# A hybrid encoder layer: value tiles in the pool of the FFN's activations, two gates as a pair at the joint, attention outputs on the other side of memory

## The chip, the core and the metric

The kernel runs on one core of a Trainium2 chip. The core has a matrix engine (PE, its weight loads PEld), a vector engine (DVE), an activation engine (ACT), a general engine (POOL) and a queue engine (SP). Each takes its instructions in the order in which they were written; they wait for each other by semaphores. SP and POOL issue the transfers (DMA) between the device's memory and the 128 partitions of the core's own memory, and a waiting transfer holds back all that stands behind it on its engine. The metric is the device time of one execution in microseconds. Of the kernel before, three runs took 1272.62, 1275.5 and 1276.87 us, so the median is 1275.5 us.

## The reference

One encoder layer over 512 tokens of 1024 features, in float32:

```python
x = x + 0.5 * swiglu(rmsnorm(x, ffn1_norm), w1, w3, w2)     # FFN a, 2816 hidden
h = rmsnorm(x, mix_norm)
proj = h @ w_in                 # q, k, v of attention A | q, k, v of attention B | gates
o_a = dilated attention, 24 heads of 64 in 3 groups (dilation 1, 4, 16), relative bias,
      the groups combined by their softmax denominators
o_b = attention with 8 query heads of 128 and 2 key heads, normalised q and k, rotary
merged = sigmoid(g_A) * (o_a @ w_branch_a) + sigmoid(g_B) * (o_b @ w_branch_b)
x = x + merged @ w_out
x = x + 0.5 * swiglu(rmsnorm(x, ffn2_norm), ...)            # FFN b
return rmsnorm(x, final_norm)
```

## The kernel before

The 512 tokens stand as columns, the features in eight tiles of 128 partitions (x0 to x7). Every product keeps float32 precision: an operand is split into a rounded part H and a remainder L, and `mm3` (L254) makes three matmuls of them, H·H, H·L and L·H. A weight tile of 512 KB is loaded raw (wr; wt, wa and ws for the Strassen products), ACT rounds it (wh<-..., L241), and DVE takes the remainder (wl<-..., L242). A product of one weight tile with all tokens ("feature piece", `feat`, L266) takes 24 matmuls of 512 columns. A part of the FFNs and of the projection uses Strassen's scheme (`strassen`, L308): a group of four blocks becomes seven products (A11, S1, S2, A12, S3, S4, A22) of 24 matmuls of 256 columns each. For S1 and S3 the raw weight wt is the sum of two blocks, and the second is added by a transfer that accumulates, issued on POOL (L223); for S2 and S4 DVE adds two tiles (ws<-..., L240).

PE's instructions stand in the order of the program. Other engines' instructions are placed by a scheduler, within the dependences. Tiles live in pools that are opened and closed like brackets; a pool opened where another lay waits, tile by tile, for the last reader of what lay there.

The stages in order: FFN a; the projection for attention A ("sw", ten tiles of q and k as five groups f = 0, 2, ..., 8 and the values as three groups f = 10, 12, 14) with a gate piece ahead of it; attention A with the remaining projection pieces woven in as filler (`stream`, L642; `weave`, L390); attention B with more filler; the branch products and the output projection (wo); FFN b.

**Joint 1**, FFN a to the projection. FFN a's last product, over the tiles d in the order ROWS = (0, 4, 1, 5, 2, 6, 3, 7), adds to x[d]; then ACT makes hH[d] (L398) and DVE hL[d] (L399), the normalised operand without the factor 1/rms, and the squares are summed in acc. `then(gp)` runs the projection (`project_qk`, L722) while the FFN's pools are still open. It starts with the first gate through `feat`, k = 0 to 7, whose result stays in its bank. Then follow the product A11, `stat_r` (L418, the sum of acc over the partitions, and the power -0.5 on POOL, L416), the next product, and `stat_R` (L427), which spreads the factors to R; then the gate is scaled and stored to `gate_d`.

**Joint 2**, the projection to attention A. The evictions write q and k to the device's memory `qk_d` (L746) and the values to `v_d` (L762), through two staging tiles qo. The groups of values come last (f = 10, 12, 14). `mixer` then opens a pool V (two value tiles, on the right), the pool oA of attention A's outputs, and the pool A, with the third value tile, the q and k tiles of a head pair (qk) and the probabilities. `fetch(0)` (L685) loads q and k of the first head pair, and `fetch_v` (L687 to L690) the three value tiles of 1 MB, all on POOL's queue. SP loads the bias tables W (L823, L824). Head pair by head pair, `scores_a` makes S on PE (L850) and P = S + W with its row maximum MX on DVE (L855); `values_a` follows a pair later.

**FFN b's opening.** The output projection's operands mH and mL lie in the pool M. FFN b's pools open behind it. Before, its raw weights wt and wa lay where attention A's and B's tiles had lain, apart from mH and mL.

Of the kernel before, what the change touches and what calls it, by code (L numbers as in the profile page):

```python
# [24 lines left out]
NSQ = 10  # L25
NSW = NSQ + 6
# [12 lines left out]
T = 512  # L39
# [34 lines left out]
class Layer:  # L74
    def __init__(self, ctx, tc, a):
# [34 lines left out]
        for kind, n in self.items:  # L110
            if kind == "sw":
                self.order += [("swq", at) for at in self.slots(range(0, NSW, 2), True)]
# [65 lines left out]
    def offset(self, n):  # L178
        name, key = self.order[n][:2]
        if name[:2] == "sw":  # L180
            return 160 - 128 * (n % 2)
        if name == "w2b" and key >= (NF + GROUPS["b"][2]) // 2:
            return 96
        return 160 if name in ("w2a", "w2b", "wpa", "wpb", "wo") else 224
# [91 lines left out]
    def pair(self, name, done):  # L276
        ws = [self.weights(name, c) for c in range(2)]
        banks = [self.bank() for _ in ws]
        for k in range(NK):
            s = slice(128 * k, 128 * k + 128)  # L280
            for c, (H, L) in enumerate(ws):
                self.mm3(banks[c], H[:, s], L[:, s], self.hH[k], self.hL[k], k == 0, k == NK - 1)
                if k == NK - 1:
                    done[c](banks[c])
                yield
# [153 lines left out]
    def ffn(self, s, gin, gnext, hooks, out=None, side=None, then=None):  # L439
        with ExitStack() as ctx:  # L440
# [201 lines left out]
    def stream(self, items, held=None):  # L642
        nc = self.nc
        later = lambda fn: fn if held is None else lambda ps: held.append((fn, ps))
        for kind, n in items:
# [11 lines left out]
            elif kind == "g":  # L657

                def done(ps, j=n):
                    z = self.tmp.tile([128, T], F32, tag="t", name="z")  # L660
                    nc.vector.tensor_mul(z, ps, self.R)
                    nc.sync.dma_start(self.gate_d[j], z)

                yield from self.feat("wg", n, later(done))
# [21 lines left out]

    def fetch_v(self):  # L687
        for g in range(3):
            rows = self.v_d[g].rearrange("(m r) f -> m r f", r=4) if g else self.v_d[g].rearrange("(i p) f -> p i f", p=128)
            self.nc.gpsimd.dma_start(self.V[g], rows)  # L690
# [31 lines left out]
    def project_qk(self, gp):  # L722
        nc, cp = self.nc, self.cp
        if True:
            held = []
            for _ in self.stream(self.items[:self.head], held):
                pass
            c, turn = {}, itertools.count()
# [19 lines left out]
            def staged():  # L748
                return self.g_tile(gp, next(turn) % 2, "qo", F32)[:, :1024]

            def tokens(o, src, half, neg):
                for j in range(2):
                    i = 2 * half + j
                    out, part, rc = o[:, 256 * i:256 * i + 256], src[:, 256 * j:256 * j + 256], self.r[:, i:i + 1]
# [5 lines left out]
            def store_v(f, at, o):  # L760
                dst = self.v_d[(f - NSQ) // 2].rearrange("(i p) f -> p i f", p=128)
                nc.gpsimd.dma_start(dst[:, :, at:at + 256], o.rearrange("p (i f) -> p i f", i=4))  # L762

            def evict(f, step, ps):
# [15 lines left out]
                elif step == "S4":  # L780
                    nc.vector.tensor_add(hi, ps, hi)
                    o = staged()
                    if f >= NSQ:
                        tokens(o, lo, 0, False)
                        tokens(o, hi, 1, False)
                        store_v(f, 0, o)
                        return
# [3 lines left out]
                elif f >= NSQ:  # L791
                    o = staged()
                    tokens(o, ps, 0, True)
                    tokens(o, c2, 1, True)
                    store_v(f, 256, o)
# [6 lines left out]
            def settle():  # L802
                self.stat_R()
                for fn, ps in held:
                    fn(ps)
# [87 lines left out]
    def values_a(self, hp, P, F):  # L893
# [17 lines left out]
        for stage in range(4):  # L911
# [153 lines left out]
    def mixer(self):  # L1065
        nc, tc = self.nc, self.tc
        vctx = ExitStack()
        vp = vctx.enter_context(tc.tile_pool(name="V", bufs=1, side="right", reuse_waits="tile"))
        self.V = [vp.tile([128, 4, 512], F32, name=f"V{g}") for g in range(2)]
        fill = self.stream(self.items[self.head + 1:])  # L1070
        with tc.tile_pool(name="oA", bufs=1, reuse_waits="tile") as oa:
            self.oH = [oa.tile([128, T], F32R, name=f"oH{h}") for h in range(4)]
            self.oL = [oa.tile([128, T], F32R, name=f"oL{h}") for h in range(4)]
            with tc.tile_pool(name="A", bufs=1, reuse_waits="tile") as ap:
                self.ap = ap
                self.V.append(ap.tile([128, 4, 512], F32, name="V2"))
                self.fetch(0)
                self.fetch_v()
# [16 lines left out]
            vctx.close()  # L1095
# [188 lines left out]
```

## Time and profile before

| | |
|---|---|
| median of three runs | 1275.5 us |
| profiled execution, its own time | 1272.24 us |
| its span | 1270.5 us |
| granted PE clock, mean | 0.992 |
| bytes moved | 192.95 MB, 152 GB/s |
| DVE, ACT, POOL busy | 72%, 48%, 10% |

The span is the time from the first to the last instruction of the profiled execution; 1.7 us lie around it. A row of a timeline gives the start, the duration, the engine, the line of the kernel, the operation, and out<-in by the program's names; in brackets stands the idle time before it and what ended it. A row of windows gives, for each engine, busy time and number of instructions, then PE's granted clock, the busy share of the DMA engines and GB/s.

The chain that ended last belongs to PE nearly throughout:

```profile
PE 91%; DVE 4%; DMA 2%; issue 1%; ACT 1%; SPq 0%; POOL 0%; POOLq 0%; DVEq 0%
```

### The profile page before, as it was taken

What the parts mean: (1) busy time and instruction counts of PE and PEld (TensorE: products, weight loads), DVE (VectorE), ACT (ScalarE), POOL (GpSimd) and SP (SyncE); (2) the same over time, 40 slices, a digit from 0 to 9 for tenths busy, and PEclk for the clock granted to TensorE, in tenths of its full rate; (3) what the DMA queues carried; (4) which work ended last, traced back from release to release, by engine and by line L of the source; (5) the groups of instructions that cost most, each with busy time, mean ns of one, the idle gap of its engine ahead of it and who ended that gap; (6) DMA issues with size and microseconds to landing.
All of it is one profiled execution on the core that took longest, in us unless ns stands there. A gap on an engine that the chain in (4) does not pass through costs nothing.

```text
span 1270.5 us, 20497 instructions
## 1 busy us (share of the span) xinstructions
PE 1242.5 (98%) x8214; PEld 1107.6 (87%) x8214; DVE 917.2 (72%) x1372; ACT 605.3 (48%) x903; POOL 131.2 (10%) x139
## 2 busy tenths in 40 slices
PE   9999999999999999699999999999999999999997
PEld 7897999899889999477788878888889989988996
DVE  7784687569988886366746798856777747874775
ACT  8551354155554445354423446655465415532553
POOL 1111110001212110310000200000301000100001
PEclk9999999999999999899999999999999999999998
DMA  9875766367369873853223220147837636743222
GB/s 299 232 187 177 189 187 181 98 168 198 100 147 258 249 200 113 302 168 102 76 104 108 83 92 26 34 142 215 223 101 199 183 94 176 194 150 106 62 82 67
DMA packets 88271, 192.95 MB, mean 152 GB/s; under 512 B 12768, under 2 KB 19312, under 8 KB 87920
## 3 DMA queue, kind: packets, MB, share of 16 engines
q1 hardware_dynamic: 68336, 142.32, 33.5%
q0 software_dynamic: 19120, 48.78, 18.3%
q8 instruction: 64, 1.05, 0.3%
q10 hardware_dynamic: 720, 0.55, 0.1%
q14 instruction: 31, 0.25, 0.1%
HBM read 176.84 MB, written 18.43 MB: 154 GB/s over the span
## 4 chain that ended last, share of the span: by engine, by line
PE 91%; DVE 4%; DMA 2%; issue 1%; ACT 1%; SPq 0%; POOL 0%; POOLq 0%; DVEq 0%
PE mm L256 23%; PE mm L257 22%; PE mm L258 22%; PE Y L257 4%; PE Y L256 4%; PE Y L258 4%; PE X L256 2%; PE X L257 2%; PE X L258 2%; PE S L850 1%; PE mm L901 1%; DMA qk<-qk_d 1%; PE Tb L1040 1%; PE T L919 1%; DVE wl L242 1%
## 5 line engine op out<-in xcount | busy, mean ns | idle before, releaser
L241 ACT CAST wh<-wr 128x1024 fp32r<-128x1024 f32 x133 | 139.4, 1049 | 178.4 <-PE mm L257 126.5
L256 PE MATMUL mm<-hH,wh 128*128 128x256 f32 (+1 forms) x600 | 201.4, 336 | 2.0 <-ACT hH L398 1.9
L257 PE MATMUL mm<-hL,wh 128*128 128x256 f32 (+1 forms) x600 | 196.6, 328 | 1.1 <-DVE hL L399 1.0
L258 PE MATMUL mm<-hH,wl 128*128 128x256 f32 (+1 forms) x600 | 196.4, 327 | 0.9 <-DVE wl L242 0.9
L242 DVE TENSOR_TENSOR wl<-wr,wh 128x1024 fp32r<-128x1024 f32 x133 | 163.0, 1226 | 29.3 <-ACT wh L241 28.9
L256 PE MATMUL mm<-gg,wh 128*128 128x512 f32 (+1 forms) x376 | 141.5, 376 | 0.0
L257 PE MATMUL mm<-gg,wh 128*128 128x512 f32 (+1 forms) x376 | 141.0, 375 | 0.0
L258 PE MATMUL mm<-gg,wl 128*128 128x512 f32 (+1 forms) x376 | 141.0, 375 | 0.0
L256 PEld LDWEIGHTS mm<-hH,wh 128*128 128x128 f32 x600 | 113.4, 189 | 17.9 <-issue 3.7
L257 PEld LDWEIGHTS mm<-hL,wh 128*128 128x128 f32 x600 | 113.6, 189 | 11.6 <-DVE hL L399 2.6
L258 PEld LDWEIGHTS mm<-hH,wl 128*128 128x128 f32 x600 | 113.2, 189 | 11.9 <-DVE wl L242 1.3
L257 PE MATMUL mm<-TL,wh 128*128 128x256 f32 x384 | 106.0, 276 | 0.0
L258 PE MATMUL mm<-TH,wl 128*128 128x256 f32 x384 | 106.0, 276 | 0.0
L256 PE MATMUL mm<-TH,wh 128*128 128x256 f32 x384 | 106.0, 276 | 0.0
L241 ACT CAST wh<-wa 128x1024 fp32r<-128x1024 f32 x54 | 56.8, 1051 | 96.0 <-PE mm L257 48.3
L241 ACT CAST wh<-ws 128x1024 fp32r<-128x1024 f32 x54 | 56.8, 1052 | 76.6 <-PE mm L257 49.2
L242 DVE TENSOR_TENSOR wl<-wt,wh 128x1024 fp32r<-128x1024 f32 x54 | 66.1, 1224 | 34.5 <-ACT wh L241 33.6
L529 DVE TENSOR_TENSOR u<-mm,R 128x512 f32<-128x512 f32 (+1 forms) x52 | 33.7, 648 | 79.2 <-PE mm L258 79.0
L241 ACT CAST wh<-wt 128x1024 fp32r<-128x1024 f32 x54 | 56.8, 1052 | 67.0 <-PE mm L257 39.8
L242 DVE TENSOR_TENSOR wl<-wa,wh 128x1024 fp32r<-128x1024 f32 x54 | 67.0, 1241 | 27.5 <-ACT wh L241 27.5
L256 PEld LDWEIGHTS mm<-gg,wh 128*128 128x128 f32 x376 | 70.6, 188 | 14.1 <-PE mm L258 0.9
L258 PEld LDWEIGHTS mm<-gg,wl 128*128 128x128 f32 x376 | 70.6, 188 | 12.9
(261 smaller groups left out, 3209.2 us busy)
## 6 DMA issues: line engine op xcount, KB each, us to landing
wr<-in_w2a SPq DMA_DIRECT2D x22, 512.0 KB, 3.7
wr<-in_w2b SPq DMA_DIRECT2D x22, 512.0 KB, 3.5
wt<-in_w13b SPq DMA_DIRECT2D x20, 512.0 KB, 4.1
wa<-in_w13b SPq DMA_DIRECT2D x20, 512.0 KB, 3.4
wt<-in_w13b POOLq DMA_DIRECT2D x20, 512.0 KB, 5.8
wt<-in_w13a SPq DMA_DIRECT2D x18, 512.0 KB, 3.5
wt<-in_w13a POOLq DMA_DIRECT2D x18, 512.0 KB, 6.0
wa<-in_w13a SPq DMA_DIRECT2D x18, 512.0 KB, 3.5
```

The source lines that it names most:

```text
L241: self.nc.scalar.copy(H, raw)
L242: self.nc.vector.tensor_sub(L, raw, f32(H))
L256: mm(out, lH, rH, start=start, stop=False, skip_group_check=more)
L257: mm(out, lH, rL, start=False, stop=False, skip_group_check=more)
L258: mm(out, lL, rH, start=False, stop=stop, skip_group_check=more)
L529: nc.vector.tensor_mul(u, ps, R)
L850: nc.tensor.matmul(*args, start=True, stop=True)
L901: nc.tensor.matmul(oc, v, p, start=st, stop=sp)
L919: nc.tensor.transpose(ps[:, 128 * b:128 * b + 128], P[h][:, c0 + 128 * b:c0 + 128 * b + 128], self.ident)
L1040: nc.tensor.transpose(pt[:, 128 * j:128 * j + 128], P[h, j][:, 128 * k:128 * k + 128], self.ident)
```

## The change

It has three parts, and their tiles move in memory with them.

1. At joint 1 gates 0 and 1 run as a pair (`pair` gets the order of k as an argument, here ROWS), both results stay in their banks, `stat_r` follows directly, and after the first product `settle` makes R and scales both gates. Gate 1 leaves the filler of attention A.
2. The projection takes the values of groups 12 and 14 first, then q and k, then group 10 (`SW_Q`). The pool g, which held FFN a's activations, stays open until attention A ends (`gctx`) and holds the value tiles: V1 and V2, stored to `v_d` and read back as soon as both halves are there, and V0, which the evictions write in place. The two staging tiles become two halves of one tile. The transposed probabilities PT lie in pool g too. `fetch_v` and the pool V are gone.
3. The pool oA goes to the right end of memory; pool g lies below wx and c in both FFNs, and the tiles of the attentions lie elsewhere in consequence. FFN b's wt and wa now lie where mH and mL lie.

```diff
-NSW = NSQ + 6
+SW_Q = (NSQ + 2, NSQ + 4, *range(0, NSQ, 2), NSQ)
...
-        self.v_d = self.dram.tile([3, T, 512], F32, name="v_d")
+        self.v_d = self.dram.tile([2, T, 512], F32, name="v_d")
...
-        self.items = (gates(0, 1) + [("sw", 0)] + gates(1, 5) + [("qk", f) for f in range(NSQ, 12)]
+        self.items = (gates(0, 2) + [("sw", 0)] + gates(2, 5) + [("qk", f) for f in range(NSQ, 12)]
...
-            at[1] = at.pop(6)
+            at[1], at[2], at[3] = at.pop(6), at.pop(7), at.pop(2)
...
-    def pair(self, name, done):
+    def pair(self, name, done, ks=range(NK)):
...
-            self.wx = self.shifted(pool("wx", bufs=1), 128)
-            self.cp = self.shifted(pool("c", bufs=2), 128)
-            gp = pool("g", bufs=1)
+            if then:
+                self.gctx = ExitStack()
+                gp = self.gctx.enter_context(self.tc.tile_pool(name="g", bufs=1, reuse_waits="tile"))
+            else:
+                gp = pool("g", bufs=1)
+            self.wx = self.shifted(pool("wx", bufs=1), 64)
+            self.cp = pool("c", bufs=2)
...
-            for _ in self.stream(self.items[:self.head], held):
+            hold = lambda j: lambda ps: held.append((j, ps))
+            for _ in self.pair("wg", [hold(j) for j in range(self.head)], ROWS):
                 pass
+            self.stat_r()
+            self.V = {g: self.g_tile(gp, g, f"V{g}", F32).rearrange("p (i f) -> p i f", i=4) for g in (1, 2)}
+            both = self.g_tile(gp, 0, "qo", F32)
...
+            def values(f, at, a, b, neg):
+                g = (f - NSQ) // 2
+                if g == 0 and at == 0:
+                    self.V[0] = self.g_tile(gp, 0, "V0", F32).rearrange("p (i f) -> p i f", i=4)
+                o = staged().rearrange("p (i f) -> p i f", i=4) if g else self.V[0][:, :, at:at + 256]
+                tokens(o, a, 0, neg)
+                tokens(o, b, 1, neg)
+                if g:
+                    d = self.v_d[g - 1]
+                    nc.gpsimd.dma_start(d.rearrange("(i p) f -> p i f", p=128)[:, :, at:at + 256], o)
+                    if at:
+                        nc.gpsimd.dma_start(self.V[g], d.rearrange("(m r) f -> m r f", r=4))
...
-            hooks = {0: self.stat_r, 1: settle, 3: self.stat_p}
-            for n, _ in enumerate(self.strassen("q", range(0, NSW, 2), evict)):
+            hooks = {0: settle, 2: self.stat_p}
+            for n, _ in enumerate(self.strassen("q", SW_Q, evict)):
                 if n in hooks:
                     hooks[n]()
             self.TQ = None
+            self.PT = self.g_tile(gp, 3, "PT", F32)
...
-                pt = ap.tile([128, T], F32, tag="PT", name="PT", bufs=4)
+                at = T * (2 * (stage % 2) + h)
+                pt = self.PT[:, at:at + T]
...
-        vp = vctx.enter_context(tc.tile_pool(name="V", bufs=1, side="right", reuse_waits="tile"))
-        self.V = [vp.tile([128, 4, 512], F32, name=f"V{g}") for g in range(2)]
...
-        with tc.tile_pool(name="oA", bufs=1, reuse_waits="tile") as oa:
+        with tc.tile_pool(name="oA", bufs=1, side="right", reuse_waits="tile") as oa:
...
-                self.V.append(ap.tile([128, 4, 512], F32, name="V2"))
                 self.fetch(0)
-                self.fetch_v()
...
-            vctx.close()
+            self.gctx.close()
```

What this moves on the engines, at three places. The first is PE at joint 1, at the first gate's first matmuls; hH and hL are the eight operand tiles, mm the banks. Before:

```order
L256 MATMUL mm_3497<-hH0_97,wh_3356 128x512
L257 MATMUL mm_3497<-hL0_105,wh_3356 128x512
L258 MATMUL mm_3497<-hH0_97,wl_3357 128x512
L256 MATMUL mm_3497<-hH1_98,wh_3356 128x512
L257 MATMUL mm_3497<-hL1_106,wh_3356 128x512
L258 MATMUL mm_3497<-hH1_98,wl_3357 128x512
L256 MATMUL mm_3497<-hH2_99,wh_3356 128x512
```

Of the change:

```order
L256 MATMUL mm_3506<-hH0_97,wh_3357 128x512
L257 MATMUL mm_3506<-hL0_105,wh_3357 128x512
L258 MATMUL mm_3506<-hH0_97,wl_3358 128x512
L256 MATMUL mm_3507<-hH0_97,wh_3394 128x512
L257 MATMUL mm_3507<-hL0_105,wh_3394 128x512
L258 MATMUL mm_3507<-hH0_97,wl_3395 128x512
L256 MATMUL mm_3506<-hH4_101,wh_3357 128x512
```

Each operand tile now serves two banks, mm_3506 and mm_3507, before the next one is touched, and tile 4 comes where tile 1 came.

The second place is POOL's queue from the last groups of the projection to the first fetches of attention A (qk_d and v_d are in the device's memory, in_wav are weights). Before:

```order
L746 DMA qk_d<-qo 128x2x512 x2
L223 DMA wt<-in_wav 128x1024
L762 DMA v_d<-qo 128x4x256 x5
L690 DMA V_5404<-v_d 128x4x512
L762 DMA v_d<-qo 128x4x256
L690 DMA V_5405<-v_d 128x2048
L685 DMA qk<-qk_d 128x512 x6
L690 DMA V_5420<-v_d 128x2048
```

Of the change, the same engine from the first group of q and k on:

```order
L771 DMA v_d<-qo 128x4x256 x2
L223 DMA wt<-in_waq 128x2x512
L773 DMA V_3564<-v_d 128x2048
L223 DMA wt<-in_waq 128x2x512
L771 DMA v_d<-qo 128x4x256 x2
L223 DMA wt<-in_waq 128x2x512
L773 DMA V_3565<-v_d 128x2048
...
L747 DMA qk_d<-qo 128x2x512 x2
L223 DMA wt<-in_wav 128x1024
L747 DMA qk_d<-qo 128x2x512 x4
L687 DMA qk<-qk_d 128x512 x20
```

The loads of V now stand among the projection's accumulating weight transfers, there are two instead of three, and the fetches of qk follow the stores of qk directly.

The third place is DVE at FFN b's opening, from the last tile of the sum of squares on; ms<-stat takes the statistics, T, TH and TL are Strassen's sums of the operand. Before:

```order
L409 TENSOR_TENSOR acc<-acc,sq 128x512
L366 TENSOR_TENSOR T_9263<-T_9263 128x1024
L415 TENSOR_SCALAR ms<-stat 128x4
L242 TENSOR_TENSOR wl<-wr,wh 128x1024
L366 TENSOR_TENSOR T_9263<-T_9264,T_9263 128x1024
L359 TENSOR_TENSOR TL<-T_9263,TH 128x1024
```

Of the change:

```order
L409 TENSOR_TENSOR acc<-acc,sq 128x512
L366 TENSOR_TENSOR T_9208<-T_9208 128x1024
L415 TENSOR_SCALAR ms<-stat 128x4
L240 TENSOR_TENSOR ws<-wt,wa 128x1024
L242 TENSOR_TENSOR wl<-wr,wh 128x1024
L366 TENSOR_TENSOR T_9208<-T_9209,T_9208 128x1024
L359 TENSOR_TENSOR TL<-T_9208,TH 128x1024
```

The sum ws<-wt,wa, which before stood 28 rows earlier, among the output projection's last tiles, now stands behind the statistics, and the next weight split and the sums T wait behind it.

More of the change, by code (lines that the diff above doesn't have):

```diff
@@ L111, in __init__ @@
             if kind == "sw":
-                self.order += [("swq", at) for at in self.slots(range(0, NSW, 2), True)]
+                self.order += [("swq", at) for at in self.slots(SW_Q, True)]
                 continue
@@ L640, in bias_spread, with gate_done, stream @@
             self.nc.gpsimd.dma_start(self.zd[h], bass.AP(tensor=src.tensor, offset=src.offset, ap=[[0, 128], [1, NV]]))
-    def stream(self, items, held=None):
+    def gate_done(self, ps, j):
+        z = self.tmp.tile([128, T], F32, tag="t", name="z")
+        self.nc.vector.tensor_mul(z, ps, self.R)
+        self.nc.sync.dma_start(self.gate_d[j], z)
+    def stream(self, items):
         nc = self.nc
-        later = lambda fn: fn if held is None else lambda ps: held.append((fn, ps))
         for kind, n in items:
@@ L657, in stream @@
             elif kind == "g":
[L659 to L664, printed above, removed]
+                yield from self.feat("wg", n, lambda ps, j=n: self.gate_done(ps, j))
             elif kind == "pa":
```

38 lines of the change are left out of this document (13 added, 25 removed).

## The prediction

> **What bounds the kernel now.** I read the page's busy times first, then the waits of PE, then the two stretches that those waits name, in the timelines of single engines.
>
> ```profile
> PE 1242.5 (98%) x8214; PEld 1107.6 (87%) x8214; DVE 917.2 (72%) x1372; ACT 605.3 (48%) x903; POOL 131.2 (10%) x139
> PE S L850 <- DMA qk<-qk_d: 11.4, 1, 11.4
> PE mm L256 <- ACT hH L398: 1.9, 2, 1.0
> PE S L850 <- DVE MX L855: 1.6, 2, 1.4
> PE mm L257 <- DVE hL L399: 1.0, 2, 0.5
> ```
>
> PE is busy for 98% of the 1270.5 us. The number of matmuls stays as it is, so all that can be won is idle time of PE, and time that it spends at a lower clock. The waits (us in total, times, longest) stand in two places. One is the joint between the first FFN and the projection (hH, hL: 2.9 us by this view). The other is the joint between the projection and the first attention (qk 11.4 us, MX 1.6 us).
>
> **Joint 1, by rows.** PE around the first gate:
>
> ```profile
> 344.73 0.39 PE L256 MATMUL mm<-gg,wh 128*128 128x512 f32 x1
> 346.77 0.39 PE L256 MATMUL mm<-hH,wh 128*128 128x512 f32 x1
> 349.97 0.51 PE L256 MATMUL mm<-hH,wh 128*128 128x512 f32 x1 [0.96 <-ACT hH L398]
> 354.65 0.50 PE L256 MATMUL mm<-hH,wh 128*128 128x512 f32 x1 [0.97 <-ACT hH L398]
> 356.26 0.28 PE L256 MATMUL mm<-hH,wh 128*128 128x256 f32 x1
> ...
> 357.62 0.28 PE L256 MATMUL mm<-hH,wh 128*128 128x256 f32 x1
> ```
>
> Between 344.73 and 346.77 lie nine matmuls of 512 columns, so one takes 0.227 us and a gate's 24 take 5.44 us. The first gate begins at 346.77 and the Strassen product after it at 356.26: 9.49 us for 5.44 us of work. **Lost: 4.05 us.** (The last two rows are twelve matmuls of 256 columns apart: 0.1133 us each. They serve a rival below.) The gate takes its k tiles as 0, 1, ..., 7, while DVE makes them in the order 0, 4, 1, 5, 2, 6, 3, 7. Its last two come here, and then the sum of squares:
>
> ```profile
> 350.09 0.74 DVE L399 SCALAR_TENSOR_TENSOR hL<-x,par,hH 128x512 fp32r<-128x512 f32 x1
> ...
> 354.89 0.74 DVE L399 SCALAR_TENSOR_TENSOR hL<-x,par,hH 128x512 fp32r<-128x512 f32 x1
> 355.56 0.68 DVE L409 TENSOR_TENSOR acc<-acc,sq 128x512 f32<-128x512 f32 x1
> ```
>
> These are tiles 3 and 7, ready at 350.83 and 355.63. After the change two gates run side by side in DVE's order: six matmuls, 1.36 us, for each k. From 346.77 on, tile 3, seventh in order, is wanted at 346.77 + 6 x 1.36 = 354.93, four us after it is ready, and tile 7 at 356.29, 0.66 us after it is ready. So PE doesn't wait, and the pair ends at 346.77 + 10.88 = 357.65. That is 1.39 us later than the first gate alone ended before, with 5.44 us more done. **Gain: 5.44 - 1.39 = 4.05 us.** Below it lies 0 (if DVE is held up as much as PE runs ahead); it can't be more than the 4.05 us that are lost. I take 4.0. DVE keeps its order up to tile 7 but for which weights it splits in two places. The statistics come directly behind the pair, and one product of 2.72 us covers them:
>
> ```profile
> 360.21 1.99 POOL L416 TENSOR_TENSOR r<-ms,mhalf 128x4 f32<-128x4 f32 x1
> ```
>
> POOL's power takes 1.99 us, and DVE's row ahead of it must come first, so some 0.2 us may be left before the transposes. The two gates' products with R now stand together on DVE; the weights of three steps are ready ahead of them.
>
> **Joint 2, by rows.** First POOL's queue, then the chain that ended last, then the landing times of qk:
>
> ```profile
> 511.20 0.75 POOL L762 DMA_DIRECT2D v_d<-qo  x1 [8.55 <-ACT qo L758]
> 512.09 0.75 POOL L690 DMA_DIRECT2D V<-v_d  x1
> 513.00 0.75 POOL L762 DMA_DIRECT2D v_d<-qo  x1 [0.16 <-issue]
> 513.75 0.55 POOL L690 DMA_DIRECT2D V<-v_d  x1
> 514.85 2.15 POOL L685 DMA_DIRECT2D qk<-qk_d  x4 [0.55 <-DMA wr<-in_waq]
> ```
> ```profile
> 515.40 13.15 DMA qk<-qk_d
> ```
> ```profile
> DMA to landing us min/median/max: 8.3/12.9/13.7
> ```
>
> The fetch of the first head pair (qk) stands behind the last stores of the values and two loads of 1 MB each, V0 and V1. It is issued only when the projection has run out, and lands 13.15 us later. Four windows show what that costs: PE busy, granted clock, DMA share and GB/s.
>
> ```profile
> 516.00:529.00 13.00, 1.62 (x8) 1.11 (x8) 1.92 (x2) 1.04 (x1) 3.84 (x8) 0.74 1.02 377
> 529.00:542.00 13.00, 13.00 (x84) 8.84 (x82) 6.99 (x38) 8.30 (x27) 3.56 (x7) 0.87 0.84 276
> 542.00:556.00 14.00, 12.39 (x74) 8.80 (x73) 6.89 (x35) 7.38 (x31) 1.60 (x3) 0.88 0.67 208
> 579.00:591.00 12.00, 12.00 (x94) 8.64 (x91) 8.90 (x40) 7.92 (x27) 1.06 (x2) 1.00 0.29 90
> ```
>
> The last window, at head pair 2, is the same work undisturbed: no idle PE, clock 1.00. In the other three PE is idle for 13.00 - 1.62 = 11.4 us and 14.00 - 12.39 = 1.6 us. At clocks of 0.74, 0.87 and 0.88 it also loses about 1.62 x 0.26 + 13.00 x 0.13 + 12.39 x 0.12 = 3.6 us. **Sum: 16.6 us.** The 1.6 us at head pair 1 is the bias table W, which comes through the same engines:
>
> ```profile
> 541.43 5.33 DMA W<-zd
> ```
> ```profile
> DMA to landing us min/median/max: 2.2/4.7/12.2
> ```
>
> Over the four head pairs W lands in 2.2 us at best and 12.2 us at worst (the second answer), and the worst is at the first pair, beside the V loads. After the change none of the three V loads stands here: V1 and V2 are read back in the middle of the projection, and V0 is written in place without a store or a load (2 MB of traffic less). POOL's queue goes from the last qk stores straight to the fetches. These need memory that the wt tiles held, so they wait for the last casts of those:
>
> ```profile
> 495.17 1.05 ACT L241 CAST wh<-wt 128x1024 fp32r<-128x1024 f32 x1 [1.29 <-PE Y L258]
> ```
>
> In the time of before that is 496.2, against 514.85 for the issue now. Even with the longest landing of 13.7 us the tiles are there by 510, and PE wants them at about 517: its 11.4 us of waiting end with the landing at 515.40 + 13.15 = 528.55. So the 11.4 us go. The later clock and W follow if no idle time is left. W of the first pair is now queued ahead of a gate's store, but it is still wanted at once: I keep 0.6 us for it. **Gain: 16.0 us**; bounds 11.4 (only the fetch's wait goes) and 16.6.
>
> On the clock, the Trainium skill ("TensorE: Matmul & The Clock Gate", "What's actually happening") says that the array is throttled after an idle window of some 3.4 us. The second dip here (0.88) stands behind only 1.6 us of idle time. By that rule it could have a cause of its own and stay; by the rows, which show 1.00 at pair 2, it goes. The difference would be 1.5 us (12.39 x 0.12), a rival below.
>
> **What else moves.** The stores of V are in the first third of the Strassen products instead of the last, and two loads of 1 MB come with them:
>
> ```profile
> 370.00:420.00 50.00, 50.00 (x443) 50.00 (x443) 43.10 (x46) 23.11 (x27) 10.00 (x11) 1.00 0.92 238
> 450.00:500.00 50.00, 50.00 (x434) 50.00 (x433) 36.73 (x42) 26.02 (x34) 5.10 (x7) 1.00 0.50 142
> ```
>
> With q and k the DMA share was 0.92, with the values 0.50, and PE had no idle time in either. The two kinds change places, so the values' 0.50 now takes the loads; 2 MB at 238 GB/s is 8.8 us of transfer spread over two groups of seven products, 19 us each (7 x 24 x 0.1133). I count nothing; bounds 0 and 8.8 us, if weights behind them on POOL come late.
>
> The second FFN's opening gets tighter. Its tiles wt and wa now lie where mH and mL lie, which the output projection reads to its end. Their first loads, which stood between those of that projection's weights, now stand behind them all and wait for its matmuls. DVE's sum ws<-wt,wa, which stood early, now stands right behind the statistics, and DVE's whole queue waits for it. The rows that price this (the second answer is a group of weight splits, the fourth the landing of wt between 870 and 960):
>
> ```profile
> 930.56 0.16 DVE L415 TENSOR_SCALAR ms<-stat 128x4 f32<-128x4 f32 x1 [0.54 <-PE stat L423]
> ```
> ```profile
> L242 DVE TENSOR_TENSOR wl<-wr,wh 128x1024 fp32r<-128x1024 f32 x133 | 163.0, 1226 | 29.3 <-ACT wh L241 28.9
> ```
> ```profile
> wt<-in_w13b SPq DMA_DIRECT2D x20, 512.0 KB, 4.1
> ...
> wt<-in_w13b POOLq DMA_DIRECT2D x20, 512.0 KB, 5.8
> ```
> ```profile
> DMA to landing us min/median/max: 3.3/6.4/14.3
> ```
> ```profile
> 921.01 12.20 SPq L220 DMA_DIRECT2D wr<-in_w13b  x3
> ```
> ```profile
> 947.26 0.28 PE L256 MATMUL mm<-hH,wh 128*128 128x256 f32 x1
> ```
>
> The first wt load follows a wr load of about 921.0, say at 921.5. With median landings wt is whole at 921.5 + 4.1 + 1 (POOL's issue, an estimate from the 0.75 us above) + 5.8 = 932.4, two us after the ms row, and ws is made by 933.6. Some 9.3 us of DVE rows stand from there to the first Strassen weights (seven of 128x1024 at 1.23 us, one of 128x512 at 0.68 us), which makes 942.9, and PE wants them at 947.26. So nothing is lost. With the longest landing on the second transfer alone it is 951.4, 4.1 us late; with both at their longest, 14.4 us. I take 0, the value of the medians.
>
> **Sum.** 4.0 + 16.0 = 20.0 us off the profiled execution's 1272.2 us (span 1270.5 and 1.7 around it): 1252.2. The median shown, 1275.5, lies 3.3 above that execution, so the like median after is **1255.5 us**.
>
> **Rivals, with chances.** Faster or slower counts from 0.3% (3.8 us), about what a measurement tells from no change.
> - Forecast, both joints mended, 1251 to 1259: **0.58**. For it: the rows give dates, with margins of 0.66 us at joint 1 and about 7 us at joint 2.
> - Joint 2 half mended: only the 11.4 us go, because W still comes late and the clock dips again. 1275.5 - 4.0 - 11.4 = 1260: **0.12**. The second dip alone staying (the rule above): 1257, **0.07**.
> - FFN b's opening late through DVE's queue, 1255.5 + 4.1 = 1260, at most 1270: **0.10**. For it: several 512 KB loads start together. Against: the margin of 4.4 us just worked out.
> - Weights late while V is reloaded: up to 1255.5 + 8.8 = 1264: **0.04**.
> - It doesn't do what it says: the fetch's wait is replaced by one as long, for the memory or the queue, and joint 1 stays DVE's: within 0.3% of 1275.5, **0.05**.
> - Slower: PE's pace depends on where tiles lie. With the values' products every second step is slower, as these rows, 24 matmuls apart, show:
>
> ```profile
> 481.04 0.28 PE L256 MATMUL X<-wh,hH 128*128 128x256 f32 x1
> ...
> 483.87 0.28 PE L256 MATMUL mm<-wh,hH 128*128 128x256 f32 x1
> ```
>
> That is 0.1179 us a matmul against 0.1133, 4.1%. Nearly every tile outside the constants moves. If all of PE's 1242.5 us took that pace it would be +51 us, 1306. It outweighs the gain by 0.3% from 24 / 51, about half of PE's work. Against it: the wt, wa and ws tiles keep their places relative to each other. **0.04.**
>
> Faster 0.91, same 0.05, slower 0.04. The range 1250 to 1266 holds the forecast nearly whole, the halves and most late openings, some 0.85; the far ends (1270, 1275, 1306) are left out.
>
> **What would show it.** Joint 1: no idle PE at hH or hL in the pair, 10.9 us long, with the transposes of r at most some tenths late. Joint 2: no wait of S for qk, PEclk 1.00 through pairs 0 and 1, W landing in 2 to 5 us. FFN b: DVE's ws made before 938 in the time of before. I am wrong if a wait of PE over 2 us stands in one of these places, or if a count of matmuls in 10 us elsewhere falls.

## The result, and the profile after

The changed kernel takes **1266.2 us** (median of four runs, 1265.17 to 1266.36), the kernel before, beside it, 1274.5 us (four runs, 1272.62 to 1276.87): ratio 0.9932, 95% interval 0.9913 to 0.9951. It is faster, but by 8.3 us, where 20 were forecast. The profiled executions stand at 1272.24 and 1266.25 us, so between the two traces 6.0 us went, and 14.0 us of the forecast are to be found.

The span falls into stages, each of which begins with the same matmul in both traces. Head pairs are counted from 0, so pair 2 is the third; where an expectation below gives a stretch up to "the second pair's first S", it means this S. The dates are starts of PE's rows; "forecast" is the length before, less the prediction's terms (the second gate, 5.44 us, moves from the third stage to the first).

| from | to | before | forecast | after | missing |
|---|---|---|---|---|---|
| first gate, 346.77 / 346.92 | first S, 528.64 / 520.60 | 181.87 | 171.9 | 173.68 | 1.8 |
| first S | S of pair 2, 579.55 / 574.33 | 50.91 | 46.3 | 53.73 | **7.4** |
| S of pair 2 | attention B's first Tb, 753.80 / 744.62 | 174.25 | 168.8 | 170.29 | **1.5** |
| Tb | last mH product, 923.87 / 915.06 | 170.07 | 170.1 | 170.44 | 0.4 |
| last mH product | FFN b's product X, 955.64 / 949.89 | 31.77 | 31.8 | 34.83 | **3.1** |
| X | end of the span, 1270.47 / 1264.47 | 314.83 | 314.8 | 314.58 | -0.3 |

With 0.15 us ahead of the first gate, that is 14.0. The 11.4 us of joint 2 came, and in the stage behind it 7.4 us of the forecast are missing: it is 2.8 us longer than it was. The rest is lost in places that the forecast held to be free. The waits of PE say which (us in total, times, longest):

```profile
PE S L857 <- DVE MX L862: 5.2, 2, 4.7
PE mm L256 <- ACT c L497: 1.6, 1, 1.6
PE mm L256 <- DVE oL L952: 1.4, 1, 1.4
...
PE Y L258 <- DVE wl L242: 0.9, 1, 0.9
PE mm L256 <- ACT c L786: 0.7, 1, 0.7
```

The waits for qk and hH are gone from the list. Those of S for MX stood at 1.6 us before; the c of L497, oL and the wl of Y are new. At joint 1, PE's timeline shows the pair, from its first matmul to the sum that follows it:

```profile
346.92 0.39 PE L256 MATMUL mm<-hH,wh 128*128 128x512 f32 x1
...
357.84 0.95 PE L423 MATMUL stat<-ones,acc 128*128 128x1 f32 x8
...
374.14 0.39 PE L256 MATMUL mm<-wh,TQ 128*128 128x256 f32 x1 [0.68 <-ACT c L786]
```

The pair takes 10.92 us, the forecast 10.88. The one new wait behind it is 0.68 us at the fifth product.

At joint 2, POOL's timeline, and the rows of PE's with the first S of pair 0 and three of pair 1's:

```profile
505.20 0.72 POOL L747 DMA_DIRECT2D qk_d<-qo  x1 [3.86 <-DVE qo L741]
505.92 4.29 POOL L687 DMA_DIRECT2D qk<-qk_d  x8
512.36 0.54 POOL L687 DMA_DIRECT2D qk<-qk_d  x1 [2.14 <-DMA qk<-qk_d]
```
```profile
520.60 1.13 PE L857 MATMUL S<-qk 64*128 64x256 f32 x8
...
531.21 1.14 PE L857 MATMUL S<-qk 64*128 64x256 f32 x8
...
537.00 0.48 PE L857 MATMUL S<-qk 64*128 64x128 f32 x2 [0.48 <-DVE MX L862]
542.19 2.07 PE L857 MATMUL S<-qk 64*128 64x128 f32 x14 [4.71 <-DVE MX L862]
```

The fetch is issued at once behind the last store, 9 us earlier than before, and S begins without a wait. Pair 1 then stands still for 5.2 us, and the windows (busy PE, granted clock, DMA share) show a second price:

```profile
530.00:540.00 10.00, 7.00 (x40) 4.30 (x38) 3.96 (x15) 4.50 (x17) 2.96 (x6) 1.00 0.75 228
540.00:550.00 10.00, 7.81 (x42) 6.22 (x43) 5.74 (x37) 5.92 (x25) 0.54 (x1) 0.66 0.28 67
550.00:560.00 10.00, 10.00 (x55) 8.29 (x55) 9.11 (x26) 4.84 (x12) 0.00 (x0) 1.00 0.56 159
```

At 0.66, 7.81 us of busy PE lose another 2.7 us: 5.2 + 2.7 is the 7.4 and the 0.6 that the forecast allowed for W. MX waits for P<-S,W, and that for W. DVE's timeline, and SP's:

```profile
536.16 0.42 DVE L862 CUSTOM_DVE_ANT_0 P<-S,W 128x256 f32<-128x256 f32 x1 [2.38 <-DMA W<-zd]
...
541.36 0.43 DVE L862 CUSTOM_DVE_ANT_0 P<-S,W 128x256 f32<-128x256 f32 x1 [4.42 <-DMA W<-zd]
```
```profile
529.26 0.37 SPq L878 DMA_DIRECT2D d<-SO  x1
529.72 1.16 SPq L880 DMA_DIRECT2D d<-SO  x2
530.97 0.54 SPq L830 DMA_DIRECT2D W<-zd  x1
535.39 0.33 SPq L882 DMA_DIRECT2D SO<-d  x1
535.77 0.75 SPq L831 DMA_DIRECT2D W<-zd  x1
536.61 0.41 SPq L649 DMA_DIRECT2D gate_d<-z  x1
537.07 0.43 SPq L830 DMA_DIRECT2D W<-zd  x1
537.54 0.43 SPq L831 DMA_DIRECT2D W<-zd  x1
```
```profile
DMA to landing us min/median/max: 2.5/4.1/5.9
```

W lands in 2.5 to 5.9 us, about as quickly as forecast (the last row, for 505 to 560). But three of its four pieces for pair 1 are issued only at 535.8 to 537.5, 4.6 to 6.3 us after the pair's first S. There are two W tiles, which pair 0 reads to its last P, so the first piece can't go out before 531. Then SP's queue stands until 535.39 at SO<-d, the second half of a small round trip: each pair stores its sums SO to memory and reads them back in another order, before `scores_a` merges them to F.

FFN b, on DVE and then on PE:

```profile
928.66 1.23 DVE L240 TENSOR_TENSOR ws<-wt,wa 128x1024 f32<-128x1024 f32 x1 [6.75 <-DMA wt<-in_w13b]
```
```profile
942.56 0.38 PE L258 MATMUL Y<-TH,wl 128*128 128x256 f32 x1 [0.87 <-DVE wl L242]
...
947.04 0.38 PE L256 MATMUL mm<-TH,wh 128*128 128x256 f32 x1 [1.63 <-ACT c L497]
```

DVE's queue stands for 6.75 us at the sum ws, and PE feels it 14 and 18 us later.

### The profile page after: what moved, and what is told of

Its sections match the earlier page's. It is cut to its first block, busy times and chain, and to the rows that moved or that the text cites. A ratio compares the mean times of both kernels' runs of the same rounds, so it can differ in the third digit from the quotient of the medians.

```text
span 1264.5 us, 20486 instructions
## 1 busy us (share of the span) xinstructions
PE 1241.8 (98%) x8214; PEld 1107.9 (88%) x8214; DVE 911.7 (72%) x1372; ACT 605.2 (48%) x903; POOL 132.9 (11%) x136
## 4 chain that ended last, share of the span: by engine, by line
PE 88%; DVE 5%; DMA 2%; ACT 1%; issue 1%; POOL 1%; SPq 0%; POOLq 0%; DVEq 0%; ACTq 0%
PE mm L256 22%; PE mm L258 21%; PE mm L257 21%; PE Y L258 4%; PE Y L257 4%; PE Y L256 4%; PE X L258 2%; PE X L257 2%; PE X L256 2%; PE S L857 1%; DVE wl L242 1%; PE mm L908 1%; PE Tb L1048 1%; DMA wt<-in_w13b 1%; PE T L927 1%
```

## The experiments

The state to start from: pair 1 loses 7 us through W's late issue (theory "queue") or through slow landings beside the fetches of qk (rival "traffic"); FFN b loses 3.1 us through ws on DVE's queue. Most of these kernels have one time alone, and the kernel before by itself ranges from 1271.16 to 1278.03 us, so they are judged by the stage lengths of their traces, like those in the table.

Stage lengths vary too. Where the program of a stage is that of the changed kernel, the traces here differ: first gate to first S takes 173.68 to 174.34 us in seven of them, first S to S of pair 2 takes 52.26 to 54.34 us in five, and last mH product to X takes 33.96 to 35.05 us in nine. From S of pair 2 to Tb it is 170.26 to 170.31 us in ten. A difference that stays within these bounds shows nothing.

**1. W of pair 1 issued earlier, still two tiles.** The loads are put into a function `bias_tiles` and called for pair 1 ahead of pair 0's SO transfers:

```diff
+        if hp == 0:
+            self.bias_tiles(1)
         d0 = self.dram.tile([T, 4], F32, name=f"d0_{hp}")
```

> The bias tables W of head pair 1 are issued on SP ahead of the SO transfers of pair 0, still into two tiles, so still behind pair 0's last reads of them. Of the change, from the first S (520.6) to the first S of pair 2 (574.3) it is 53.7 us, with 5.8 us of idle PE and a clock of 0.66 behind it; undisturbed it would be about 45.7. Theory 'queue': W is late because SP waits for the round trip of SO (4.4 us) between W's pieces. Then all four pieces are issued within 2 us, land in about 5 us, the wait of S falls from 5.2 us to under 1.5 us, and the stretch to 46 to 48.5 us. Rival 'traffic': W is late because the transfer engines are full with qk. Then the four land together in 8 to 10 us, the wait stays at 3 to 5 us, and the stretch at 51 to 54 us.

Measured: 1263.2 us, stage 51.28 us instead of 53.73. SP's timeline:

```profile
531.09 0.54 SPq L829 DMA_DIRECT2D W<-zd  x1
531.69 0.42 SPq L830 DMA_DIRECT2D W<-zd  x1
532.20 0.92 SPq L829 DMA_DIRECT2D W<-zd  x1
533.21 0.60 SPq L649 DMA_DIRECT2D gate_d<-z  x1
533.87 0.64 SPq L830 DMA_DIRECT2D W<-zd  x1
```

The last piece is issued 3.7 us earlier, and the wait of S falls to 3.0 us. By its numbers the rival comes out: wait and stage lie at the low end of its ranges, and the last piece has landed 9.2 us after the first is issued. It takes 6.4 us instead of 4.0, so of the 3.7 us only 1.3 are left when it lands. The order on SP costs something, since 51.28 is 1.0 us below the shortest stage of that program. What is left is the tiles, whose first piece goes out at 531 in either, or slow landings; this run doesn't tell which.

**2. Four W tiles, those of pairs 0 and 1 loaded at the start.**

```diff
-            w = ap.tile([128, T], F32, tag="W", name="W", bufs=2)
+            w = self.ap.tile([128, T], F32, tag="W", name="W", bufs=4)
...
                 self.fetch(0)
+                self.bias_tiles(0)
+                self.bias_tiles(1)
```

> Four tiles for W instead of two; those of pairs 0 and 1 are loaded together before pair 0. Both theories on W give no wait of S at pair 1 and a clock of 1.00 behind it: the stretch from the first S to the first S of pair 2 falls from 53.7 us to 45.5 to 47 us. A third theory, that pair 1 waits for something else (DVE itself, or qk), leaves a wait of 2 us or more with W long landed.

Measured: 1261.8 us, stage 49.73, above the 45.5 to 47 that both theories on W give. No wait of S is left, so it was W that held pair 1. The third theory comes out in part: a new wait, for DVE, stands behind it (PE's waits, then DVE's timeline):

```profile
PE T L930 <- DVE P L918: 2.6, 2, 1.7
```
```profile
545.79 0.18 DVE L890 TENSOR_TENSOR MN<-SO 128x16 f32<-128x16 f32 x1 [5.77 <-DMA SO<-d]
```

DVE reaches pair 0's merge (MN) and stands there 5.77 us for SO's round trip; behind it in the queue are pair 1's maxima and the scaling of pair 0's P, which PE's transposes T read.

**3. The merge of every pair behind the next pair's last maxima,** on top of run 2 (the merge becomes a function, and its first instruction is pinned):

```diff
+        def merge():
+            with self.tc.issue_after(self.maxima.ins):
                 nc.vector.tensor_tensor(MN, SO[:, 0, :, 0:2], SO[:, 1, :, 0:2], op=ALU.min)
```

> The four bias tiles of the earlier run, and in addition the merge of the two halves' sums (MN to F) stands on DVE behind the next head pair's last maxima, so that DVE no longer waits for the round trip SO<-d ahead of P. Theory 'DVE held by the round trip': the wait of PE's transposes for P (2.6 us with four tiles alone) goes, the clock stays at 1.00 from 530 to 570, and the stretch from the first S to the second pair's first S is 46 to 47.5 us (49.7 with four tiles alone, 53.7 in the changed kernel). Rival 'traffic' (what is left of the loss is P's own lateness, since W lands late among the fetches): the wait for P stays or goes over to S for MX, stretch 48.5 to 50. Rival 'the merge is late': the first products of o (oL, F) wait for DVE at the third pair, over 1 us of wait there.

Measured: 1272.0 us. The stage is 46.94 us, as the theory has it, and the price follows at once:

```profile
PE T L935 <- DVE P L923: 8.6, 3, 3.8
```

One wait of 1.2 us stands at the first pair, and 3.8 and 3.6 us at the next two, at 583 and 619, with clocks of 0.68 and 0.50 over the four us behind them. The late merge helps at the first pair, where DVE stood for the round trip, and costs at the next two. The rival named the wrong place: it is T that waits, not the products of o.

**4. The late merge for pair 0 alone,** and with it a kernel of everything (runs 2, 4, 9 and 10):

> Four bias tiles, and the merge of the sums set back on DVE behind the next pair's last maxima for the first head pair alone; pairs 1 to 3 merge where they did. Theory 'the late merge is right at the first pair, where the round trip SO<-d is slow, and wrong at the others, where it is fast': the stretch from the first S to the second pair's first S is 46.5 to 47.5 us as in the run before, the waits of 4 us for P at 579 and 614 are gone, and the time from the gate's start to the last PE instruction is about 903.5 us (906.3 with four tiles alone, minus 2.8). Rival 'any merge that is set back is paid for in the next pair': waits for P of over 2 us at the second pair's values, no better than with four tiles alone.

> All of it together: four bias tiles, the first pair's merge set back, the first sum of the second FFN behind the split of S1 on DVE, the values' weights at one offset. If the losses stand in places apart, the gains add: 6.8 (pairs 0 and 1) + 3.1 (second FFN) + 0.6 (values' weights) = 10.5 us off the changed kernel, so 1266.2 - 10.5 = 1255.7 us, which is what the prediction gave for the changed kernel itself. Rival 'the places are coupled' (what is won ahead turns into a wait later, as the cover missing at attention A's end did): 1258 to 1262.

Measured: 1273.5 us, and 1269.9 us for all together (six runs; ratio to before 0.9956, 0.9940 to 0.9972). Both theories missed, and so did the rival of the second (1258 to 1262); the rival of the first foresaw waits for P, but not the long one that came at pair 0's values. The first kernel's stage is 60.59 us. Its wait on PE, then its row on DVE:

```profile
PE T L939 <- DVE P L927: 13.3, 1, 13.3
```
```profile
558.65 0.28 DVE L895 TENSOR_TENSOR MN<-SO 128x16 f32<-128x16 f32 x2 [8.60 <-DMA SO<-d]
```

The "x2" tells it: both pairs' merges stand side by side. As I wrote it, pair 1's merge came ahead of pair 0's, so DVE waited 8.60 us for pair 1's round trip, which nobody wanted yet, with pair 0's scaling behind it.

**5. The merges in the order in which their data come,** with everything else, and the same without any merge moved:

```diff
+        if hp == 1:
+            self.late[1].append(self.late[0](self.maxima))
+        if hp < 2:
+            self.late = merge, res
+        else:
+            res.append(merge())
...
+            if hp == 0 and stage == 2:
+                self.late[1].append(self.late[0](self.scaled))
```

> As the run before, with the merges in the order in which their data come: the first pair's behind the second pair's last maxima, the second pair's behind the last scaling of the first pair's P. Theory 'what failed was only that DVE met the second pair's merge, and its round trip, first': no wait of PE for P above 2 us, stretch from the first S to the second pair's first S 46.5 to 48 us, time 1255 to 1257 us. Rival 'a merge that waits for a round trip holds PE wherever it stands in DVE's queue': a wait of several us for P or for qk's eviction between 550 and 566, time 1259 to 1266.

> Four bias tiles, the first sum of the second FFN behind the split of S1, the values' weights at one offset; every merge stands where it stood. If these three add: 4.5 (four tiles) + 3.1 (second FFN) + 0.6 (values' weights) = 8.2 us off the changed kernel, 1258.0 us. Rival 'they are coupled': 1260 to 1263.

Measured, four runs each: **1255.6 us** (1254.49 to 1257.54; ratio to before 0.9849, 0.9834 to 0.9863) and 1258.1 us (1257.34 to 1258.78; ratio 0.9864, 0.9848 to 0.9881). Both totals lie on their theories, and the first is the fastest kernel here. In the second that is partly luck: four tiles brought 3.1 us (stage 50.67) where 4.5 were counted, and the stretch from the gate to the first S fell by 1.6 us where 0.6 were. The windows of the first, then what is left of the wait for P in the first and in the second:

```profile
530.00:540.00 10.00, 10.00 (x75) 7.10 (x76) 7.52 (x35) 8.70 (x33) 2.21 (x5) 1.00 0.83 287
540.00:550.00 10.00, 9.02 (x44) 7.25 (x43) 7.03 (x25) 5.07 (x14) 0.00 (x0) 1.00 0.41 103
```
```profile
PE T L947 <- DVE P L935: 1.0, 1, 1.0
PE T L935 <- DVE P L923: 3.1, 2, 2.2
```

In the first the stage is 46.71 us against 46.3 forecast, at full clock, though the DMA share of 0.83 is higher than in the changed kernel. So the traffic by itself doesn't cost the 7 us.

**6. The values last again,** with V0 still written in place and the pools as changed:

```diff
-SW_Q = (NSQ + 2, NSQ + 4, *range(0, NSQ, 2), NSQ)
+SW_Q = (*range(0, NSQ, 2), NSQ + 2, NSQ + 4, NSQ)
```

> Only the order of the projection's groups is changed back, so that the values come last (q and k first, then groups 12, 14, 10): the stores and reloads of V1 and V2 stand right ahead of the fetch of the first head pair on POOL's queue. Theory 'queue' (the 11.4 us at joint 2 came from the fetch standing behind the values' stores and reloads): the fetch is issued 5 to 12 us later than in the changed kernel (505.9) and S waits for qk by 1 to 8 us. Rival 'place' (it came from V lying in the pool of attention A and being fetched as 3 x 1 MB at the joint; without V0's load the fetch is early enough in any order): no wait of S for qk above 0.5 us. The stretch from the first S to the second pair's first S says what the reloads cost head pair 0 and 1: 53.7 us in the changed kernel; by the traffic theory 54 to 58, by the theory that W's order alone decides, 53 to 54.

Measured: 1268.9 us. POOL's timeline:

```profile
510.24 0.55 POOL L773 DMA_DIRECT2D V<-v_d  x1 [3.38 <-issue]
510.78 3.81 POOL L687 DMA_DIRECT2D qk<-qk_d  x7
```

The fetch is 4.9 us later, and S still doesn't wait for it: the rival is right. V0 written in place and the new place of V1 and V2 suffice to end the 11.4 us; which of the two does it was not tried. The order of the groups is worth something in the next stage (55.62 us, 1.3 above the longest of the five, in the range of the traffic theory). Up to the first S it shows nothing (174.41).

**7. One gate at joint 1,** gate 1 back in the filler:

```diff
-        self.items = (gates(0, 2) + [("sw", 0)] + gates(2, 5) + [("qk", f) for f in range(NSQ, 12)]
+        self.items = (gates(0, 1) + [("sw", 0)] + gates(1, 5) + [("qk", f) for f in range(NSQ, 12)]
...
-            for _ in self.pair("wg", [hold(j) for j in range(self.head)], ROWS):
+            for _ in self.feat("wg", 0, hold(0)):
```

> Part 1 undone alone: one gate through feat at the first joint in the order 0..7, gate 1 back in the filler of attention A. Theory 'pair' (the pair's cover is worth 4.05 us there, paid back in part because a gate is missing as filler at attention A's end): the first gate takes 9.5 us again for 5.44 us of matmuls, the wait of PE for oL at the last values of attention A (1.4 us in the changed kernel) is gone, and the stretch from the gate's start to the first Tb, with equal work in it, comes out 2 to 3 us longer than in the changed kernel (397.70 us there). Rival 'cover is no scarce good' (nothing is paid back): 4 us longer. Rival 'the pair brings nothing, DVE holds it up': no longer.

Measured: 1267.0 us. The gate's first matmul and the sum behind it, on PE:

```profile
347.21 0.39 PE L256 MATMUL mm<-hH,wh 128*128 128x512 f32 x1
...
356.12 1.05 PE L423 MATMUL stat<-ones,acc 128*128 128x1 f32 x8
```

The gate takes 8.91 us, so the pair is worth 5.44 - (10.92 - 8.91) = 3.4 us there; up to the first S (171.35 us) 2.5 to 3.1 are left, by the bounds above. The wait for oL is gone. From S of pair 2 to Tb it is 174.25 us, so the missing gate shortens that stage by 3.96 us and not by 5.44: 1.5 us, about half of the gain, are paid back. From the gate's start to the first Tb the kernel needs 399.09 us, 1.4 longer than the changed one: less than expected, in the theory's direction.

**8. One more gate ahead of attention B's pieces,** to fill the hole at attention A's end:

```diff
-                      + gates(5, 12) + [("b", g) for g in range(3)] + gates(12, 16) + [("pa", 0)])
+                      + gates(5, 13) + [("b", g) for g in range(3)] + gates(13, 16) + [("pa", 0)])
```

> One more gate piece (gate 12) as filler before attention B's projection, so that attention A's last values have one behind them again; one fewer follows in attention B. Of the change PE waits 1.4 us for oL at 656 (pitch 1.68 against 0.23). Theory 'filler': that wait goes, and the stretch from attention A's last value matmul to the first transposes of attention B grows by the gate's 5.44 us less 1.5, while the end comes 1 to 1.5 us earlier. Rival: the wait moves into attention B, which now has one piece less, and the end stays within 0.5 us.

Measured: 1266.3 us, its span 0.1 us longer. The wait for oL is gone, and this one has grown, from 0.3 to 0.6 us in the traces without the move, on PE in attention B:

```profile
751.66 0.33 PE L1048 MATMUL Tb<-ident,Pb 128*128 128x128 f32 x1 [1.24 <-DVE Pb L1042]
```

From S of pair 2 to the last mH product it is 339.91 us; in the ten traces with the pair and without the move it is 340.3 to 340.8 (run 3, with its late merges, left out). So some 0.5 us are won, not the 1.4 of the wait: most of the hole has moved with the gate.

**9. The values' weights at one offset.** In the function that places tiles:

```diff
+        if name == "swq" and key[0] >= NSQ:
+            return 160
```

> Only the place of weights: the raw and rounded weights of the values' groups all lie at offset 160 of 256 words instead of 160 and 32 in turn. Theory 'pace by place' (a product of 256-column matmuls whose moving weights lie at 32 beside stationary operands at 224 takes 2.83 us instead of 2.73): the 22 slow products become fast ones, the values' groups take 21 products x 2.73 us, and the first S stands 1 to 2 us earlier counted from the gate's start (173.68 us in the changed kernel). Rival 'pace by neighbours or by DMA traffic': the slow products stay slow, no change of over 0.3 us.

Measured: 1264.2 us; 173.05 us from the gate to the first S instead of 173.68. Of the matmuls of 256 columns between 357 and 520, 412 begin 116 to 125 ns after the one ahead of them, 579 in the changed kernel and 378 before. The same product in the changed kernel and in this one:

```profile
407.88 0.28 PE L256 MATMUL X<-hH,wh 128*128 128x256 f32 x1
...
410.71 0.28 PE L256 MATMUL mm<-hH,wh 128*128 128x256 f32 x1
```
```profile
408.03 0.28 PE L258 MATMUL X<-hH,wh 128*128 128x256 f32 x1
...
410.75 0.28 PE L258 MATMUL mm<-hH,wh 128*128 128x256 f32 x1
```

It is 2.83 us and 2.72. So a tile's place does bear on the pace: three other traces that leave the places as they were (runs 1, 8 and 10) count 579 or 580. But seven slow products' worth went, not all 22. The two kernels of run 5 have the same offset, and four W tiles, and count 297 and 204, so the rule as I put it is not the whole of it, and what else decides stays open. The gain is 0.6 to 1.3 us, by the bounds above.

**10. The first ws of FFN b behind S1's split on DVE,** nothing else:

```diff
+            with ExitStack() as pin:
+                if name == "swb" and key == (GROUPS["b"][0], "S2"):
+                    pin.enter_context(self.tc.issue_after(self.split_ins.ins))
+                self.nc.vector.tensor_add(raw, a, b)
```

> Only the order of DVE at FFN b's opening: the sum ws<-wt,wa of the first group stands behind the split of S1's weights; memory, transfers and their order stay. Of the change, from the last mH matmul to the first X it is 34.8 us, before 31.8, and DVE stands 6.75 us for wt. Theory 'DVE queue': the 3.06 us are lost since all of DVE's work waits behind that row; with it moved the stretch is 31.7 to 32.3 us. Rival 'late weights': wt and wa themselves come too late for S1 and S2, because their loads start behind the output projection; then 34 to 35 us stay, with PE waiting for wl or wh of wt or ws.

Measured: 1261.9 us; from the last mH product to X 31.77 us, what it was before and is in all four kernels with this edit, instead of 34.83. The sum now stands where its data have long landed:

```profile
935.98 1.22 DVE L243 TENSOR_TENSOR ws<-wt,wa 128x1024 f32<-128x1024 f32 x1
```

## Why the prediction was right or wrong

- **Joint 1, 4.0 us: right in its place, and then paid back.** The pair ran as worked out (10.92 us for 10.88) without a wait for hH or hL above 0.3 us. The failing step is a term put at nothing without a reason: what the moved gate covered where it came from, in attention A. Without it PE waits 1.4 us for oL there, and that stage is 1.5 us longer than forecast. By run 7 part 1 as a whole is worth 1.0 to 1.6 us. The 0.4 us of attention B are no such cost: eight of the ten other traces with the pair in that place take 170.06 to 170.12 us there, and the kernel before takes 170.07. 0.7 us went at the fifth product, for c.
- **Joint 2, the 11.4 us: right, but its margin came by luck.** The prediction lets the fetches wait for the last casts and dates them 496.2 in the time of before. They waited for the last store of qk and went out at 505.92, which is some 502.6 in that time, six us later. Pair 0's six tiles landed in 6.1 to 7.5 us instead of 13.7, so the last stood ready some 4.5 us ahead of S, where about 7 were named: two errors that nearly cancel. Run 6 corrects the reason: the fetch is early enough in either order of the groups.
- **Joint 2, W and the clock, 1.6 + 3.6 - 0.6 us: wrong, and this is half of what was missed.** The step that failed is "the later clock and W follow if no idle time is left", with 0.6 us kept for W. I judged W by its landing times, which came out as I thought, and never asked when it is issued: for pair 1 only when pair 0 has let go of the two tiles, and behind SO<-d on SP. With PE on time, pair 1's S begins 9.8 us earlier (541.02 to 531.21), but the last piece of W is issued only 6.2 us earlier (543.76 to 537.54). Runs 1, 2 and 5 show three holds, one behind the other: SP's order (53.73 to 51.28), the tiles (to 49.73), DVE held by the round trip (to 46.71). Their order and their sum of 7 us are shown; the single prices are not, since traces of one program differ by 2 us here, four tiles give 50.67 in the second kernel of run 5, and in run 1 slower landings took part. The rival "Joint 2 half mended" named W and allowed for no more than the old loss; the stage grew from 50.91 to 53.73.
- **The clock.** The dip followed the wait as forecast: 0.66 behind 4.7 us, none where the wait went (run 5). The rival by the Trainium skill ("TensorE: Matmul & The Clock Gate", "What's actually happening"), that the second dip has a cause of its own, falls in that run. What the page says, half the clock behind an idle window of some 3.4 us, agrees with the 4.7 us here, behind which 0.51 was granted (the last row). Shorter idle time is another matter. Before the change 1.6 us of it, in the first row, stood ahead of 0.57, in the second; by the page's window alone that dip would not be there, and the measurement decides.

```profile
545.00:549.00 4.00, 2.39 (x17) 1.63 (x17) 2.07 (x12) 0.40 (x1) 1.07 (x2) 1.00 1.08 370
549.00:553.00 4.00, 4.00 (x22) 2.84 (x21) 2.48 (x16) 3.93 (x18) 0.00 (x0) 0.57 0.33 106
```
```profile
544.00:548.00 4.00, 4.00 (x16) 2.77 (x16) 2.22 (x13) 4.00 (x20) 0.00 (x0) 0.51 0.13 4
```

- **V moved, 0: 0.8 us.** No weight came late; but more products ran at the slow pace (run 9).
- **FFN b, 0: 3.1 us.** The mechanism was named with a chance of 0.10, and the term was mis-sized: by median landings ws would be made by 933.6 in the time of before, with 4.4 us to spare behind it. It was made at 929.9, which is 938.7 in that time, 5.1 us later. wt, issued at 912.75, landed in 5.7 us instead of 4.1, and its second half, issued on POOL at 919.06, in 9.6 us instead of 5.8, among nine loads of 512 KB that SP issued between 912.20 and 918.20. My own bounds had a long second landing at 4.1 us. The median was not the likely value here, where several loads start together.
- **The total.** Forecast 20 us, measured 8.3. With the holds taken away, and the values' weights moved (run 5), the change gives 19.5 us by the medians and 17.7 by the profiled executions (1272.24 to 1254.49). That the first is so near to 20 is partly luck: 0.6 us or more of it come from run 9's place, which no term of the forecast holds. The 2.3 us that are then still missing stand in the first stage (0.6), at pairs 0 and 1 (0.4) and at attention A's end (1.5).

## What to carry to other kernels

When a wait is removed, list what the next stage needs and ask of each item when it is issued and what holds it (a tile not yet free, a queue behind a waiting transfer, an engine standing at a round trip), not only how long it takes to land: here a gain of 11 us was followed by a wait of 5 one stage later. Work that fills a hole has a second value as cover where it came from, so a moved piece is priced at both places. On an engine that takes its work in order, an instruction that waits for a transfer belongs behind all that is wanted sooner, and two such belong in the order in which their transfers end.

## What the hardware showed that was not expected

- Idle time of 1.4 us at 656 and of 0.9 and 1.6 us at 942 and 947 left the clock at 1.00. In run 2, 2.6 us in two pieces between 548 and 552 came with 0.80 there and 0.77 over the next four us, and before the change 1.6 us stood ahead of 0.57 over four. Length alone doesn't decide it; what else does was not tried.
- A store of 8 KB can take as long as a large transfer. SO<-d waits for d<-SO on SP. In the changed kernel the two are issued 2.51 us apart at pair 3 (617.84 and 620.35, DMA share 0.46) and 4.08 at pair 1 (553.22 and 557.30, share 0.95 in the first of these us); at pair 0 of run 2 they stand 7.85 us apart (534.93 and 542.78, share 1.07 up to 540).
- A product of 24 matmuls takes 2.72 or 2.83 us in the same kernel, 4% apart; an offset moved turned some of the slow ones into fast ones (run 9).
